# Six instead of eight heads of the recurrent layer computed ahead by Strassen's scheme, with reloads on GpSimd's queue and four gates in the recurrence's buffers

## The chip, the core and the metric

The kernel runs on one NeuronCore of a Trainium2 chip. TensorE (PE in the profile) multiplies matrices into PSUM, VectorE (DVE) and ScalarE (ACT) work element by element, GpSimd (POOL) and SyncE (SP) mostly issue DMAs. Each engine works through its own list of instructions strictly in order, and waits on semaphores for the others. The metric is the device time of one execution in microseconds (us).

## The reference, cut to what matters

A trunk of two residual layers runs over 528 positions (16 meta tokens and 512 inputs) of width 2048, in float32. Layer 0 is a convolution module beside a sparse attention; the change leaves its arithmetic alone. Layer 1 is a gated linear recurrence with 16 heads of width 128:

```python
def odd_mixer(hn, w_in, lb, norm_g, w_out):
    q, fz, i, g = split_last(hn @ w_in, (D_REC, D_REC, D_REC, D_REC))
    log_f = jnp.logaddexp(jnp.log(lb), jnp.log1p(-lb) + jax.nn.log_sigmoid(fz))
    k = (1.0 - lb) * jax.nn.sigmoid(-fz)
    o = hgrn2_chunkwise(heads(jax.nn.silu(q)), heads(log_f), heads(k), heads(i))
    o = o * lax.rsqrt(jnp.mean(jnp.square(o), -1, keepdims=True) + RMS_EPS)
    o = o * norm_g.reshape(H_C, DV_C).astype(jnp.float32)
    o = o.reshape(bsz, t_len, D_REC).astype(hn.dtype) * jax.nn.silu(g)
    return o @ w_out
```

So each head needs three projections of the normed input (its forget gate `fz`, its query `q`, its value `i`, called `v` in the kernel), then its recurrence; the output gate `g` is a fourth projection per head, and all heads go through one output projection.

## The kernel before, in words

**Products.** Every projection takes 128 output columns, a *stripe*, over 16 blocks of 128 inputs. A float32 operand is split into a high and a low part, and each block costs three matmuls: high by high (L177), weight high by input low (L178), weight low by input high (L179). The weights of half a stripe (8 blocks, 512 KB) come by one load: a DMA from SP into a staging tile `w32`, of which there are two (L144, `load_half`), then ScalarE rounds them to `wh` (L148) and VectorE takes the rest as `wl` (L149); there are three `wh` and three `wl`. A *wide* stripe covers all 528 positions in two parts of 264 columns: 2 halves x 2 parts x 8 blocks x 3 = 96 matmuls. A *narrow* stripe covers the 512 inputs with 48 matmuls of 512 columns.

**The stages of layer 1, in order of the program.**
1. The output projection of layer 0: 16 wide stripes. Behind each, VectorE adds the residual (L701), the sum goes to DRAM as `h1d` (L714), and the scaled sum `hg` becomes the input X1 of layer 1, split in two. For n >= 8, VectorE forms sums of two `hg` that Strassen's scheme needs, and two DMAs store them as `x1d` (L728, L729).
2. The Strassen stage. `fz` and `v` of the even heads are computed ahead for all positions: two stripes of the same head (a *pair*) times two halves of the positions form a 2x2 block product, done with 7 products of 24 matmuls (264 columns) instead of 8. Eight pairs give 56 products. Three sums of inputs, the forms N2, T3 and T4, come back from `x1d` through 24 reloads into three buffers `fr` (`reload`, L752), and are split by ScalarE (L189) and VectorE (L190); 8 more reloads restore X1 at the end. The products of pairs 0 to 2 run in the order (1, 5, 2, 3) for each pair, then all 6, 7 and 4, so N2 is first used by the 13th product, T3 by the 16th, T4 by the 19th. The sums of weights (four per pair) are made earlier, in DRAM, by copies and accumulating DMAs that are spread over layer 0 (`some_steps`, L241 and L243). The finished `fz` and `v` go to DRAM as `fvd` from GpSimd's queue (L803). Every third weight load of this stage, counted from its first, goes through a third staging tile `w33` (`strassen_weights`), which lies in the stage's own pool `fap`, in memory that other tiles held before.
3. The recurrence, head by head (`rec_head`). Even heads load `fz` and `v` back (L1011, L1012) and need only the narrow stripe of `q`; odd heads run three stripes. A head's own work on TensorE is many small matmuls (L859 to L861, L889, L893, L964 to L982, L993, L994) that wait for ScalarE and VectorE in a long chain; the stripes of later heads stand between them and fill the time. GpSimd clears a tile `vt` per head (L892), which waits until the head before the previous one has done its last L982, and then issues four DMAs of the sums for the output projection (L241, L243).
4. The 16 gates of layer 1, narrow stripes (`gate_on`): VectorE takes each from PSUM (L185), the result multiplies the head's output. Their tiles `gt2` lie in the pool `fp`, which opens when the recurrence's pool `hr` closes and takes its memory.
5. The output projection, 56 Strassen products of 256 columns, each load again through `strassen_weights`, with `w33` now in `fp`.

**What sets the order.** A scheduler builds each engine's list from priorities (`band`: weights before evacuations before the recurrence, stripes last) and its own estimate of when things are ready; a load that it expects to wait for memory can stand ahead of loads that are needed sooner.

Of the kernel before, what the change touches and what calls it, by code (L numbers as in the profile page):

```python
# [10 lines left out]
F32 = mybir.dt.float32  # L11
# [7 lines left out]
SEQ = 512  # L19
NM = 16  # L20
T = SEQ + NM
# [51 lines left out]
def trunk_kernel(ctx: ExitStack, tc: tile.TileContext, x: bass.AP, w: bass.AP, wukv: bass.AP,  # L73
# [171 lines left out]
    def product_weights(pair, m):  # L245
# [3 lines left out]

    PAIRS = [(S_FQV + 3 * h, S_FQV + 3 * h + 2) for h in range(0, 16, 2)]  # L250
    plain_steps = [("copy", m, pr) for pr in PAIRS for m in (7, 5)]
    steps = [(what, m, pr) for g in (0, 4)
             for what, m in (("add", 7), ("add", 5), ("copy", 6), ("add", 6), ("copy", 3), ("add", 3))
             for pr in PAIRS[g:g + 4]]

# [438 lines left out]
    for n in (8 * j + i for i in range(8) for j in range(2)):  # L694
# [26 lines left out]
        if n >= 8:  # L721
            with band(SIDE):

                a, b = first_hg, hg
                V.tensor_tensor(b[:, RT], b[:, RT], a[:, RT], op=OP.subtract)
                V.scalar_tensor_tensor(a[:, LT], b[:, RT], -1.0, a[:, LT], op0=OP.mult, op1=OP.subtract)
                V.scalar_tensor_tensor(b[:, LT], a[:, LT], -1.0, b[:, LT], op0=OP.mult, op1=OP.subtract)
                Q.dma_start(x1d[n - 8], a)  # L728
                Q.dma_start(x1d[n], b)  # L729
        if tap and n in (0, 15):  # L730
# [19 lines left out]
    def reload(i, sl):  # L750
        src = fap.tile([128, HT], F32, name="fr", bufs=3)
        Q.dma_start(src, x1d[i, :, sl])  # L752
        return src
# [9 lines left out]

    loads = [0]

    def strassen_weights(pair, m, pool):
        loads[0] += 1
        return load_half(product_weights(pair, m),
                         w32=pool.tile([128, 1024], F32, name="w33", bufs=1) if loads[0] % 3 == 0 else None)

    turns = [(p, m) for ms in ((1, 5, 2, 3), (6,), (7,), (4,)) for p in range(3) for m in ms]
    turns += [(p, m) for p in range(3, 8) for m in (1, 5, 2, 6, 7, 3, 4)]
    U, C = {}, {}
    for at, (pr, m) in enumerate(turns):
# [5 lines left out]
        with band(WGT):  # L780
            hi, lo = strassen_weights(PAIRS[pr], m, fap)
        products(o, hi, lo, forms1[FORM[m]], True, True)
# [247 lines left out]

    hr.__exit__(None, None, None)
    fp = ctx.enter_context(tc.tile_pool(name="fp", bufs=2, side="left", reuse_waits="tile"))
    HS = SEQ // 2
# [25 lines left out]

    def gate_on(h, ps):  # L1060
        t = gt2()
        g, th = t[:, :SEQ], t[:, SEQ:]
        with band(EVAC):
# [24 lines left out]

    for i in range(8):
        for h, forms_of in ((i, forms_of_first), (8 + i, forms_of_both)):  # L1090
            gate_on(h, stripe(S_G + h, X1, wide=False))
            with band(SIDE):
                forms_of(i)
    with band(SIDE):
# [69 lines left out]
    for at, (pr, m) in enumerate(turns):  # L1164
# [7 lines left out]
        with band(WGT):  # L1172
            hi, lo = strassen_weights(OPAIRS[pr], m, fp)
        issued = products(o, hi, lo, forms[FORM[m]], True, True)
# [123 lines left out]
```

## Time and profile before

| what | value |
|---|---|
| time, median of 3 runs (lowest, highest) | 1982.93 us (1981.18, 1988.01) |
| the profiled execution's own time | 1983.95 us |
| its span, first to last instruction | 1982.2 us |
| TensorE busy | 97% of the span |
| VectorE, ScalarE busy | 71%, 46% |
| mean granted TensorE clock | 0.988 |

The profile is of one execution. A row of a timeline has the start in us, the duration in us, the engine, the line, the operation, output<-inputs, shapes, the count, and in brackets the idle time before it and what ended that. A row of waits has engine and line, who released it, then us in total, times, and the longest. A row of a table of stretches has, for each engine, its busy us with the number of instructions in brackets, then the granted clock, the DMA share and GB/s; a few per cent of matmul records are missing from such counts.

### The profile page before, as it was taken

What the parts mean: (1) busy time and instruction counts of PE and PEld (TensorE: products, weight loads), DVE (VectorE), ACT (ScalarE), POOL (GpSimd) and SP (SyncE); (2) the same over time, 40 slices, a digit from 0 to 9 for tenths busy, and PEclk for the clock granted to TensorE, in tenths of its full rate; (3) what the DMA queues carried; (4) which work ended last, traced back from release to release, by engine and by line L of the source; (5) the groups of instructions that cost most, each with busy time, mean ns of one, the idle gap of its engine ahead of it and who ended that gap; (6) DMA issues with size and microseconds to landing.
All of it is one profiled execution on the core that took longest, in us unless ns stands there. A gap on an engine that the chain in (4) does not pass through costs nothing.

```text
span 1982.2 us, 36659 instructions
## 1 busy us (share of the span) xinstructions
PE 1921.8 (97%) x14806; PEld 1797.7 (91%) x14806; DVE 1409.3 (71%) x2685; ACT 903.2 (46%) x1603; POOL 163.5 (8%) x266
## 2 busy tenths in 40 slices
PE   9999999999999999998999999999999987999997
PEld 8999899999999999998999889988888866888997
DVE  6699989987375454444766877878878876558776
ACT  6332442234436433333534655556565653325554
POOL 1000001122230200000000200001000100000000
PEclk9999999999999999999999999999999997999999
DMA  6434335677774744444766745446454531326555
GB/s 229 149 120 141 123 105 130 163 175 184 180 190 129 186 135 162 157 166 143 255 224 205 213 137 160 129 123 165 118 160 108 161 101 54 96 90 203 186 189 172
DMA packets 96889, 308.05 MB, mean 155 GB/s; under 512 B 12432, under 2 KB 24248, under 8 KB 95696
## 3 DMA queue, kind: packets, MB, share of 16 engines
q1 hardware_dynamic: 75840, 228.16, 34.8%
q0 software_dynamic: 20592, 77.36, 17.4%
q8 instruction: 116, 1.90, 0.4%
q14 instruction: 53, 0.43, 0.1%
q10 hardware_dynamic: 288, 0.19, 0.0%
HBM read 277.91 MB, written 86.98 MB: 184 GB/s over the span
## 4 chain that ended last, share of the span: by engine, by line
PE 87%; issue 5%; DVE 3%; DMA 3%; ACT 1%; POOL 1%; SPq 0%; DVEq 0%; POOLq 0%; ACTq 0%
PE mps L177 22%; PE mps L178 22%; PE mps L179 22%; PE s L177 3%; PE s L179 3%; PE s L178 3%; DMA L<-bdram 2%; PE po L600 1%; PE s L860 1%; PE s L859 1%; PE s L861 1%; PE s L575 1%; DMA L<-mask 1%; PE po L981 1%; PE po L982 1%
## 5 line engine op out<-in xcount | busy, mean ns | idle before, releaser
L177 PE MATMUL mps<-xh,wh 128*128 128x264 f32 (+2 forms) x3160 | 980.3, 311 | 17.9 <-ACT wh L148 6.9
L179 PE MATMUL mps<-xh,wl 128*128 128x264 f32 (+2 forms) x3160 | 979.0, 310 | 0.0
L178 PE MATMUL mps<-xl,wh 128*128 128x264 f32 (+2 forms) x3160 | 978.2, 310 | 0.0
L177 PEld LDWEIGHTS mps<-xh,wh 128*128 128x128 f32 x3160 | 597.5, 189 | 48.8 <-ACT wh L148 7.3
L148 ACT ACTIVATE wh<-w 128x1024 fp32r<-128x1024 f32 x337 | 356.4, 1058 | 592.0 <-PE mps L178 484.5
L178 PEld LDWEIGHTS mps<-xl,wh 128*128 128x128 f32 x3160 | 597.1, 189 | 29.0 <-issue 0.6
L179 PEld LDWEIGHTS mps<-xh,wl 128*128 128x128 f32 x3160 | 597.2, 189 | 27.7
L149 DVE TENSOR_TENSOR wl<-w,wh 128x1024 fp32r<-128x1024 f32 x337 | 411.9, 1223 | 184.5 <-ACT wh L148 177.5
L544 DVE SCALAR_TENSOR_TENSOR z<-u,vec,z 128x528 f32<-128x528 f32 x240 | 180.5, 762 | 2.6
L177 PE MATMUL s<-xh,wh 128*128 128x256 f32 (+1 forms) x328 | 92.7, 283 | 0.1
L178 PE MATMUL s<-xl,wh 128*128 128x256 f32 (+1 forms) x328 | 92.7, 283 | 0.0
L179 PE MATMUL s<-xh,wl 128*128 128x256 f32 (+1 forms) x328 | 92.6, 282 | 0.0
L185 DVE TENSOR_TENSOR gt<-mps,rstd 128x264 f32<-128x264 f32 (+1 forms) x80 | 38.4, 481 | 74.9 <-PE mps L179 74.0
L243 POOL DMA_DIRECT2D ws<-in_w_dram x64 | 61.9, 1046 | 98.9 <-DMA ws<-ws 62.4
L855 ACT ACTIVATE qhm<-q 128x256 f16<-128x256 f32 x128 | 51.7, 414 | 38.0 <-DVE q L957 33.2
L177 PEld LDWEIGHTS s<-xh,wh 128*128 128x128 f32 x328 | 61.9, 189 | 0.5 <-ACT wh L148 0.4
L178 PEld LDWEIGHTS s<-xl,wh 128*128 128x128 f32 x328 | 61.7, 188 | 0.6 <-issue 0.6
L179 PEld LDWEIGHTS s<-xh,wl 128*128 128x128 f32 x328 | 61.7, 188 | 0.0
L856 DVE SCALAR_TENSOR_TENSOR qlm<-q,qhm 128x256 f16<-128x256 f32 x128 | 52.5, 419 | 11.9 <-ACT qhm L855 11.3
L942 DVE COPY_PREDICATED A<-msk,s 128x256 f32<-128x256 uint8 x96 | 46.7, 487 | 12.0 <-PE s L861 11.4
L855 ACT ACTIVATE kt0h<-k 128x512 f16<-128x512 f32 (+1 forms) x64 | 33.3, 520 | 41.4 <-PE s L861 21.4
L855 ACT ACTIVATE kt1h<-k 128x256 f16<-128x256 f32 x64 | 26.9, 420 | 54.3 <-DVE k L948 27.7
(401 smaller groups left out, 2905.6 us busy)
## 6 DMA issues: line engine op xcount, KB each, us to landing
w<-in_w_dram SPq DMA_DIRECT2D x275, 512.0 KB, 3.6
ws<-in_w_dram POOLq DMA_DIRECT2D x80, 512.0 KB, 6.8
w<-ws SPq DMA_DIRECT2D x64, 512.0 KB, 4.2
ws<-ws POOLq DMA_DIRECT2D x32, 512.0 KB, 4.7
ws<-in_w_dram SPq DMA_DIRECT2D x16, 512.0 KB, 5.0
hin<-in_x_dram SPq DMA_DIRECT2D x16, 264.0 KB, 3.9
h1d<-hin SPq DMA_DIRECT2D x16, 264.0 KB, 2.0
x1d<-hg SPq DMA_DIRECT2D x16, 264.0 KB, 3.3
```

Of the source, the lines that this page charges most:

```text
L148: S.activation(uh, used, AF.Copy)
L149: V.tensor_tensor(ul, used, uh.bitcast(F32), op=OP.subtract)
L177: P.matmul(o, hi[:, ws], xh, start=start and k == 0, stop=False)
L178: P.matmul(o, hi[:, ws], xl, start=False, stop=False)
L179: issued.append(P.matmul(o, lo[:, ws], xh, start=False, stop=stop and k == 7))
L185: V.tensor_tensor(dst[:, sl.start - o:sl.stop - o], p[:dst.shape[0]], rstd[:dst.shape[0], sl], op=OP.mult)
L243: return G.dma_start(wsum[pair, m], src, accum_op=OP.add, max_dma_last_dim=4096)
L544: eng.scalar_tensor_tensor(z, u[:, j:j + T], col(V_CW + i * CW + j), z, op0=OP.mult, op1=OP.add)
L575: P.matmul(p[:nq, :s1 - s0], qh[:, q0:q0 + nq], Kh[:, s0:s1], start=True, stop=True)
L855: S.activation(hi, src, AF.Copy, scale=scale)
L856: V.scalar_tensor_tensor(lo, src, scale, hi, op0=OP.mult, op1=OP.subtract)
L942: V.copy_predicated(A.rearrange("p b (n a m) -> p b n a m", a=2, m=mm)[:, :, :, 1, :], msk[:, li - 1 + i:li + i, :].rearrange("p b (n m) - ...
```

## The change

Four edits, all of layer 1.

1. `PAIRS` holds the heads 0, 2, ... 10 only: 42 Strassen products instead of 56. Heads 12 and 14 compute `fz` and `v` with plain wide stripes, as odd heads do. The sums of weights for the two pairs go away (4 copies on SP, and on GpSimd's queue 4 copies and 8 accumulating DMAs), and the rest is made in groups of 3 pairs instead of 4.
2. The stores of `x1d`, the 32 reloads `fr`, and the loads of `fz` and `v` of the ahead-computed heads move from SP's queue to GpSimd's.
3. `w33` takes every third load, but only from the 10th of each of the two Strassen stages on (product index over 6 and a multiple of 3); before, a counter ran through both stages, and `w33` took the 3rd, 6th, ... load of the first stage, and in the second the 1st, 4th, 7th and so on.
4. The first four gates (heads 0, 8, 1, 9) are written before the recurrence's pool closes, and put their result into its tiles `fz` and `v`. Their part in the forms for the output projection stays behind the closing, as for the other twelve.

```diff
+    AHEAD = range(0, 12, 2)
+    PAIRS = [(S_FQV + 3 * h, S_FQV + 3 * h + 2) for h in AHEAD]
...
-                Q.dma_start(x1d[n - 8], a)
-                Q.dma_start(x1d[n], b)
+                G.dma_start(x1d[n - 8], a)
+                G.dma_start(x1d[n], b)
...
     def reload(i, sl):
         src = fap.tile([128, HT], F32, name="fr", bufs=3)
-        Q.dma_start(src, x1d[i, :, sl])
+        G.dma_start(src, x1d[i, :, sl])
...
-    def strassen_weights(pair, m, pool):
-        loads[0] += 1
+    def strassen_weights(pair, m, pool, at):
+
+        own = at > 6 and at % 3 == 0
         return load_half(product_weights(pair, m),
-                         w32=pool.tile([128, 1024], F32, name="w33", bufs=1) if loads[0] % 3 == 0 else None)
+                         w32=pool.tile([128, 1024], F32, name="w33", bufs=1) if own else None)
...
-        if h % 2 == 0:
+        if h in AHEAD:
             with band(EVAC):
-                Q.dma_start(fz, fvd[h])
-                Q.dma_start(v, fvd[h + 1])
+                G.dma_start(fz, fvd[h])
+                G.dma_start(v, fvd[h + 1])
...
-        if h % 2:
+        if h not in AHEAD:
             ps = stripe(S_FQV + 3 * h + 2, X1)
...
+    gates = [h for i in range(8) for h in (i, 8 + i)]
+    for h in gates[:4]:
+        gate_on(h, stripe(S_G + h, X1, wide=False), ht([128, T], F32, "fz", 2)[:, :SEQ],
+                ht([128, T], F32, "v", 2)[:, :SEQ])
+    hr.__exit__(None, None, None)
+    fp = ctx.enter_context(tc.tile_pool(name="fp", bufs=2, side="left", reuse_waits="tile"))
```

The order of TensorE, VectorE and ScalarE is the same in both kernels up to the end of layer 0, and in the recurrence the same stripes stand between the same heads up to the end of head 8.

**SP's list where the Strassen stage begins**, before. `w33_10623` is the load of the third product, `w32_10655` and `w32_10690` are those of the fourth and fifth; `hg` are the tiles that the stores read; in brackets the semaphores that a DMA waits for.

```order
L714 DMA h1d_105<-hin1_10137 128x528 [waits DMAHW5_49,DVE_49]
L144 DMA w32_10655<-ws67_3_4202 128x1024 [waits DMAHW0_49,DMASW5_49,DVE_49]
L144 DMA w32_10690<-in_w_dram 128x1024 [waits DMAHW4_49,DVE_49]
L714 DMA h1d_105<-hin1_10265 128x528 [waits DMAHW1_49,DVE_49]
L728 DMA x1d_106<-hg_10251 128x528 [waits DVE_49]
L729 DMA x1d_106<-hg_10379 128x528 [waits DMAHW2_49,DVE_49,Activation_49]
L144 DMA w33_10623<-in_w_dram 128x1024 [waits DMAHW3_49,DMAHW2_49,DMAHW5_49,DMAHW0_49,Activation_49]
L752 DMA fr_10411<-x1d_106 128x264 [waits PE_49]
```

The same place after the change; `w32_10599` is the third product's load, `w33_10829` the tenth's, and the semaphores DMASW are those of DMAs from GpSimd's queue.

```order
L144 DMA w32_10599<-in_w_dram 128x1024 [waits DMAHW0_49,DVE_49]
L144 DMA w32_10631<-ws67_3_4126 128x1024 [waits DMAHW2_49,DMASW1_49,DVE_49]
L715 DMA h1d_105<-hin1_10241 128x528 [waits DMAHW1_49,DVE_49]
L144 DMA w32_10666<-in_w_dram 128x1024 [waits DMAHW4_49,DVE_49]
L144 DMA w32_10698<-ws73_5_1223 128x1024 [waits DMAHW5_49,DMASW2_49,DVE_49]
L144 DMA w32_10730<-in_w_dram 128x1024 [waits DMAHW7_49,DVE_49]
L144 DMA w33_10829<-ws79_5_1440 128x1024 [waits DMASW6_49,DMASW5_49,DMASW7_49,DMASW4_49,DMAHW3_49,DMASW3_49,DMAHW6_49,DMASW2_49,DMASW1_49]
L144 DMA w32_10762<-ws73_3_4147 128x1024 [waits DMAHW0_49,DVE_49]
L144 DMA w32_10797<-in_w_dram 128x1024 [waits DMAHW1_49,DVE_49]
```

The third load no longer waits for the stores of `x1d` and stands ahead of the fourth; the load that waits for them is now the tenth, and the eighth and ninth are queued behind it.

**TensorE's list in the last head's recurrence**, before: `po` is the head's output in PSUM, `st` its state, the L177 row the next gate stripe.

```order
L975 MATMUL s_19411<-vt,kk 128x128
L978 MATMUL s_19417<-vt,kk 128x128
L978 MATMUL s_19423<-vt,kk 128x128
L981 MATMUL po<-q,st 128x128
L978 MATMUL s_19429<-vt,kk 128x128
L982 MATMUL po<-A,vt 128x128
L981 MATMUL po<-q,st 128x128
L982 MATMUL po<-A,vt 128x128
L981 MATMUL po<-q,st 128x128
L982 MATMUL po<-A,vt 128x128
L993 MATMUL s_19443<-sh,ones_h 128x512
L994 MATMUL s_19443<-sl,ones_h 128x512
```

After the change, the same head, from its last but one state on.

```order
L981 MATMUL po<-q,st 128x128
L982 MATMUL po<-A,vt 128x128
L177 MATMUL mps<-xh,wh 128x512
L178 MATMUL mps<-xl,wh 128x512
L179 MATMUL mps<-xh,wl 128x512
L177 MATMUL mps<-xh,wh 128x512
L178 MATMUL mps<-xl,wh 128x512
L179 MATMUL mps<-xh,wl 128x512
```

Before, TensorE has no stripe left from the middle of head 14 to the end of head 15, with 13 gates still to come behind; after, gate matmuls stand between the pieces of both heads, and 9 gates are left behind the last head.

**GpSimd's list in the recurrence**, after the change, around the clearing of `vt` for head 9 (`vt_16109`): `ws` are sums of weights in DRAM, `v_16351` is the value of head 10.

```order
L243 DMA ws139_5_15798<-in_w_dram 128x1024 [waits DMASW6_49,DMASW0_49]
L892 MEMSET vt_16109 128x128 [waits PE_49,Activation_49]
L241 DMA ws139_6_16343<-ws139_5_15798 16x8192 [waits DMASW0_49]
L1012 DMA v_16351<-fvd_107 128x528 [waits DMASW2_49,PE_49]
L243 DMA ws139_6_16343<-in_w_dram 128x1024 [waits DMASW1_49]
L241 DMA ws139_3_16346<-ws139_6_16343 16x8192 [waits DMASW4_49,DMASW3_49]
L243 DMA ws139_3_16346<-in_w_dram 128x1024 [waits DMASW4_49]
L892 MEMSET vt_16434 128x128 [waits PE_49,Activation_49]
```

The load of head 10's value, which stood among the weight loads of SP, now stands behind a clearing that waits for head 7's end, and a copy that waits for an earlier sum.

More of the change, by code (lines that the diff above doesn't have):

```diff
@@ L247, in product_weights @@
         return {1: w[pair[0], 0], 2: w[pair[0], 1], 4: w[pair[1], 1]}[m] if m in (1, 2, 4) else wsum[pair, m]
-    PAIRS = [(S_FQV + 3 * h, S_FQV + 3 * h + 2) for h in range(0, 16, 2)]
+    AHEAD = range(0, 12, 2)
+    PAIRS = [(S_FQV + 3 * h, S_FQV + 3 * h + 2) for h in AHEAD]
     plain_steps = [("copy", m, pr) for pr in PAIRS for m in (7, 5)]
-    steps = [(what, m, pr) for g in (0, 4)
+    steps = [(what, m, pr) for g in (0, 3)
              for what, m in (("add", 7), ("add", 5), ("copy", 6), ("add", 6), ("copy", 3), ("add", 3))
-             for pr in PAIRS[g:g + 4]]
+             for pr in PAIRS[g:g + 3]]
     def some_steps(todo, n, behind):
@@ L762, in trunk_kernel @@
                 forms1[name].append((hi, lo))
-    loads = [0]
-    def strassen_weights(pair, m, pool):
-        loads[0] += 1
+    def strassen_weights(pair, m, pool, at):
+        own = at > 6 and at % 3 == 0
         return load_half(product_weights(pair, m),
-                         w32=pool.tile([128, 1024], F32, name="w33", bufs=1) if loads[0] % 3 == 0 else None)
+                         w32=pool.tile([128, 1024], F32, name="w33", bufs=1) if own else None)
     turns = [(p, m) for ms in ((1, 5, 2, 3), (6,), (7,), (4,)) for p in range(3) for m in ms]
-    turns += [(p, m) for p in range(3, 8) for m in (1, 5, 2, 6, 7, 3, 4)]
+    turns += [(p, m) for p in range(3, len(PAIRS)) for m in (1, 5, 2, 6, 7, 3, 4)]
     U, C = {}, {}
@@ L780, in trunk_kernel @@
         with band(WGT):
-            hi, lo = strassen_weights(PAIRS[pr], m, fap)
+            hi, lo = strassen_weights(PAIRS[pr], m, fap, at)
         products(o, hi, lo, forms1[FORM[m]], True, True)
@@ L1029, in trunk_kernel @@
             tap("on0", ON[0])
-    hr.__exit__(None, None, None)
-    fp = ctx.enter_context(tc.tile_pool(name="fp", bufs=2, side="left", reuse_waits="tile"))
     HS = SEQ // 2
@@ L1058, in gt2, with gate_on @@
         return fp.tile([128, 2 * SEQ], F32, name="gt2", bufs=2)
-    def gate_on(h, ps):
-        t = gt2()
-        g, th = t[:, :SEQ], t[:, SEQ:]
+    def gate_on(h, ps, g, th):
         with band(EVAC):
@@ L1087, in forms_of_both @@
         V.scalar_tensor_tensor(aj, a, -1.0, aj, op0=OP.mult, op1=OP.subtract)
[L1089 to L1093, printed above, removed]
+    for at, h in enumerate(gates):
+        if at >= 4:
+            t = gt2()
+            gate_on(h, stripe(S_G + h, X1, wide=False), t[:, :SEQ], t[:, SEQ:])
+        with band(SIDE):
+            (forms_of_first if h < 8 else forms_of_both)(h % 8)
     with band(SIDE):
@@ L1172, in trunk_kernel @@
         with band(WGT):
-            hi, lo = strassen_weights(OPAIRS[pr], m, fp)
+            hi, lo = strassen_weights(OPAIRS[pr], m, fp, at)
         issued = products(o, hi, lo, forms[FORM[m]], True, True)
```

## The prediction

> **What bounds the kernel now.** First the page's table of engines:
>
> ```profile
> PE 1921.8 (97%) x14806; PEld 1797.7 (91%) x14806; DVE 1409.3 (71%) x2685; ACT 903.2 (46%) x1603; POOL 163.5 (8%) x266
> ```
>
> TensorE is the bound. The span is 1982.2 us and the profiled execution took 1983.95, 1.0 over the median of 1982.93. So two things can move the time: the number of matmuls, and the places where TensorE stands or runs slowly. I asked for stretches around the edits:
>
> ```profile
> 930.00:940.00 10.00, 5.04 (x21) 4.73 (x22) 4.53 (x6) 3.89 (x6) 0.00 (x0) 0.68 0.56 181
> 1160.00:1280.00 120.00, 120.00 (x1044) 107.94 (x1043) 95.00 (x212) 70.14 (x128) 8.87 (x15) 1.00 0.49 139
> 1436.07:1603.18 167.11, 160.60 (x1375) 140.37 (x1375) 134.58 (x303) 95.31 (x180) 14.42 (x26) 1.00 0.49 135
> 1618.00:1660.00 42.00, 21.53 (x216) 19.04 (x212) 28.36 (x68) 18.63 (x40) 0.82 (x1) 0.68 0.15 37
> ```
>
> Each row has the stretch, its length, then the busy time of TensorE, its weight loads, VectorE, ScalarE and GpSimd, and the granted clock. Early in the recurrence (1160 to 1280) TensorE has no gap; late it has small ones, and in the 42 us after 1618 it is half idle at a granted clock of 0.68. The other hole is at 930, the start of the Strassen stage. What ends the waits, first for TensorE from 1436 to 1661, then for SP's queue from 1600 to 1680:
>
> ```profile
> PE s L859 <- ACT qhm L855: 13.7, 8, 3.8
> PE mps L177 <- DVE gt L185: 2.8, 1, 2.8
> ```
> ```profile
> SPq L144 <- PE s L994: 37.0, 1, 37.0
> ```
>
> The last two heads are a chain over ScalarE, VectorE and TensorE with nothing to fill it: three gates occupy the three PSUM buffers, their tiles `gt2` lie in the recurrence's memory, and SP holds a load for the output projection (it waits 37.0 us for the last head's L994) with gate weights queued behind it.
>
> **Prices.** Weight roundings pace TensorE, one per half stripe or product; output gates pace narrow stripes; clearings of `vt` mark the ends of heads.
>
> ```profile
> 757.30 1.06 ACT L148 ACTIVATE wh<-w 128x1024 fp32r<-128x1024 f32 x1 [1.86 <-PE mps L178]
> 915.70 1.06 ACT L148 ACTIVATE wh<-w 128x1024 fp32r<-128x1024 f32 x1 [2.74 <-PE mps L178]
> 1002.21 1.06 ACT L148 ACTIVATE wh<-w 128x1024 fp32r<-128x1024 f32 x1 [1.60 <-PE mps L178]
> 1078.06 1.06 ACT L148 ACTIVATE wh<-w 128x1024 fp32r<-128x1024 f32 x1 [1.84 <-PE mps L178]
> ```
> ```profile
> 1684.57 0.69 DVE L185 TENSOR_TENSOR gt<-mps,rstd 128x512 f32<-128x512 f32 x1 [3.51 <-PE mps L179]
> 1796.50 0.69 DVE L185 TENSOR_TENSOR gt<-mps,rstd 128x512 f32<-128x512 f32 x1 [3.46 <-PE mps L179]
> ```
> ```profile
> 1148.80 0.38 POOL L892 MEMSET vt<- 128x128 f32 x1 [13.62 <-PE po L982]
> 1259.29 0.20 POOL L892 MEMSET vt<- 128x128 f32 x1 [28.63 <-PE po L982]
> 1436.07 0.20 POOL L892 MEMSET vt<- 128x128 f32 x1 [11.34 <-PE po L982]
> ```
>
> From 757.30 to 915.70 are 27 half stripes: 5.867 us each, 0.1222 per matmul of 264. From 1002.21 to 1078.06 are 26 Strassen products: 2.917 each. From 1684.57 to 1796.50 are 10 gates: 11.19 each, 0.2331 per matmul of 512. Heads 0, 3 and 8 end at 1148.80, 1259.29 and 1436.07. Between the first two stand 352 matmuls of 264 and 192 of 512 in the list, 43.0 + 44.8 us, in 110.5 us without gaps: the rest, 22.7, is three heads' own work, 7.6 each when it is covered.
>
> **The change part by part.**
>
> *Products.* 14 fewer Strassen products: 14 x 2.917 = 40.8 us out. Four wide stripes in: 384 x 0.1222 = 46.9 in. Both are TensorE time on the path. Net +6.1: taken alone, this edit loses. The weight sums that go with it lay beside TensorE work; I count nothing for them, and no wait of layer 0 is known to hang on the eight missing accumulations.
>
> *Start of the Strassen stage.*
>
> ```profile
> 921.69 0.43 DVE L701 TENSOR_TENSOR hin<-mps,hin 128x264 f32<-128x264 f32 x1 [2.49 <-PE mps L179]
> 926.71 1.05 PE L208 MATMUL s<-acc,ones_d 128*128 128x264 f32 x4
> 934.82 0.59 PE L177 MATMUL mps<-xh,wh 128*128 128x264 f32 x1 [6.46 <-ACT wh L148]
> 941.03 0.43 DVE L789 TENSOR_TENSOR on<-u,mps 128x264 f32<-128x264 f32 x1 [1.70 <-PE mps L179]
> ```
>
> The last stripe ends at 921.7, the third product at 941.0. Three products and the row sums (L208) need 3 x 2.917 + 1.05 = 9.8 of these 19.3 us; 9.5 are lost: 6.46 waiting for the third weights, the rest at the low clock behind that. The cause is the load of `w33`, which waits until the last `x1d` store has left memory that it takes over. After the change the third load uses a free `w32`. The tenth now waits for those stores, but the loads ahead of it take turns in two tiles and are therefore spread over the products before it: by then the stores (the last issued at 927.60, 3.3 us to land, both rows below) are in DRAM since about 931. The loads behind it are due from about 933. I take the whole 9.5 off.
>
> *Reloads on GpSimd.*
>
> ```profile
> 927.60 0.32 SPq L729 DMA_DIRECT2D x1d<-hg  x1
> 930.35 1.37 SPq L752 DMA_DIRECT2D fr<-x1d  x3
> 938.75 1.54 SPq L752 DMA_DIRECT2D fr<-x1d  x3
> 980.05 0.32 SPq L752 DMA_DIRECT2D fr<-x1d  x1
> ```
> ```profile
> x1d<-hg SPq DMA_DIRECT2D x16, 264.0 KB, 3.3
> fr<-x1d SPq DMA_DIRECT2D x32, 132.0 KB, 3.7
> fvd<-on POOLq DMA_DIRECT2D x16, 264.0 KB, 3.1
> ```
>
> The 4th to the 24th reload took from 938.75 to 980.05, 2.07 each through three buffers. TensorE no longer stands, so the 19th product, the first with T4, starts at 921.7 + 1.05 + 18 x 2.917 = 975.3 and wants T4's last part some 2.5 later, 977.8. From 928.3 (behind the last store on GpSimd) and three at once, the 24th is issued at 928.3 + 21 x 2.07 = 971.8, lands at 975.5 and is split by 976.5. That is 1.3 us of slack; if a turn of three buffers takes 1 us longer from GpSimd, the 24th is 7 later and TensorE waits 5.7; nothing excludes a faster turn. I take +1.5 between 0 and 5.7, nearer to 0 because GpSimd's stores of twice the size land in 3.1.
>
> GpSimd writes its DMAs' descriptors itself, and the place for a doubt is whether VectorE holds it up:
>
> ```profile
> L803 POOL DMA_DIRECT2D fvd<-on x16: 539/539/606, 973.6 to 1100.5; - x16
> ```
>
> Sixteen stores issued from GpSimd in this very stage, with VectorE busy for most of it, took 539 ns at the median and 606 at most. The Trainium skill (SBUF — State Buffer, "SBUF: two separate sides", the "DVE blocks DMA" trap) says that VectorE's two-port modes lock GpSimd out of writing descriptors and advises the queues of SyncE or ScalarE. By its figures, some 0.62 us alone and 3.1 locked out, seven turns would be up to 17 longer, an estimate that would put the sum near 1965. By the row no lockout of more than 0.07 us is seen in 16 issues, 2.1 over 32 reloads and off the path.
>
> *The recurrence's end.*
>
> ```profile
> 1508.34 1.22 DVE L149 TENSOR_TENSOR wl<-w,wh 128x1024 fp32r<-128x1024 f32 x1
> 1633.49 0.60 PE L889 MATMUL s<-ident,v 128*128 128x128 f32 x4
> 1656.84 0.55 PE L994 MATMUL s<-sl,ones_h 128*128 128x512 f32 x1 [0.23 <-DVE sl L990]
> 1660.15 0.79 PE L177 MATMUL mps<-xh,wh 128*128 128x512 f32 x1 [2.76 <-DVE gt L185]
> 1807.49 0.28 PE L177 MATMUL mps<-eh,wh 128*128 128x256 f32 x1
> ```
>
> From head 8's end to the first product of the output projection are 1807.49 - 1436.07 = 371.4 us. What stands there is 432 matmuls of 264 (52.8), 960 of 512 (223.8) and seven heads (53.2): 329.8. So 41.6 are lost to gaps, low clock and uncovered chains. After the change 384 more matmuls of 264 and seven gates in all stand between the pieces of heads 9 to 15: in the last head alone 156 narrow matmuls, 36 us, around a chain that takes 24 alone (from L889 at 1633.5 to L994 at 1656.8). Kept are the end, where the eighth gate still waits for `gt2` (2.76, and 0.5 for L993 and L994), and small gaps: before 1603 they are 6.5 us in five heads, 1.3 each, where a head has one narrow stripe to cover it; the fuller list should halve that, 0.65 x 7 = 4.6. Kept 7.9, gained 33.7 (range 24 to 38).
>
> VectorE doesn't become the bound: from 1436 to 1603 it is busy 134.6 of 167 us; four more wide stripes add 8 weight rests of 1.22 and 8 evacuations of 0.43, 13 us, to heads that get 46.9 more of stripes on TensorE.
>
> *Entry of the output projection.* `w33` used to carry the 1st, 4th and 7th load; now the first nine share two tiles, with loads of the residual between them:
>
> ```profile
> 1802.62 2.70 SPq L1170 DMA_DIRECT2D on<-h1d  x6
> 1806.18 6.15 SPq L1170 DMA_DIRECT2D on<-h1d  x7
> 1825.59 0.39 PE L177 MATMUL mps<-xh,wh 128*128 128x256 f32 x1 [0.44 <-ACT wh L148]
> ```
>
> Before, only 0.44 us is lost here, so there is no cushion. One load more stands behind each block: I take +2.0, between 0 and a product's 2.9.
>
> *The sum.* 1983.95 - 40.8 + 46.9 - 9.5 + 1.5 - 33.7 + 2.0 = 1950.4; against the median, 1.0 less: **1949 us**, 1.7% faster.
>
> **The rivals.**
>
> *The chain stays the bound (0.13).* Gates stand between the pieces, but VectorE and ScalarE serve them too, so the chains of heads 12 to 15 stretch. For it: TensorE's longest wait is on ScalarE. Against it: VectorE is busy only 28.4 of the 42 us after 1618. If half of the 33.7 goes, 1966.
>
> *The start's hole moves (0.15).* The tenth load, or reloads from GpSimd, arrive late, and ScalarE, which has the splits among the roundings, holds the weights back. If the 9.5 stays, 1959. For it: 1.3 us of slack. The Trainium skill (DMA: Bandwidth & Descriptors, "Issuing engines are not separate DMA queues") says that spreading DMAs over engines saves only issue time: by that the move itself brings nothing. I agree as far as that goes: the gain comes from the load that no longer waits, not from the queue.
>
> *Slower: the sums starve the heads (0.04).* On GpSimd a head's value now stands behind a clearing that waits for an earlier head's end, and behind accumulations that wait for one another. If each of five reloads (heads 2 to 10) held its head by over 7 us, the gain of 33.6 would be gone, and at 10 each the time is 1949 + 50 = 1999. Against it:
>
> ```profile
> 1405.10 0.21 POOL L892 MEMSET vt<- 128x128 f32 x1 [27.08 <-PE po L982]
> 1409.82 0.80 POOL L243 DMA_DIRECT2D ws<-in_w_dram  x1 [3.77 <-DMA ws<-ws]
> 1469.55 0.20 POOL L892 MEMSET vt<- 128x128 f32 x1 [26.81 <-PE po L982]
> ```
>
> Head 9's clearing is at 1405.1; the load of head 10's value stands behind one copy, so at about 1406, and its transposes come when head 9 ends, 1469.5. The lead is some 60 us, and it decides only when that is used up.
>
> *Nothing to see (0.03).* The freed matmul time falls in the recurrence and the chains take it all: +6.1 - 9.5 and no gain at the end leaves 1980.
>
> **How the numbers follow.** A measurement here tells 0.3%, 6 us, from no change. The forecast's own case has 0.65: 1943 (end gains 38, no new stalls) to 1957. The rivals at 1959 and 1966 bring the range's upper end to 1963, which leaves out half of the chain's case, the slower one and the null. Faster 0.93, same 0.03, slower 0.04.
>
> **What would show it.** Right: no gap over 2 us between 921 and 945; 2.92 us per product and 42 of them; TensorE busy over 9 tenths through the last heads at clock 1.00, one wait of about 3 us for VectorE's `gt` behind the last head, then 9 gates of 11.2 us. SP's waits show no 37 us on L994. Wrong: waits of TensorE on `qhm` of over 10 us, ScalarE waiting on `fr` for over 3 us at a time, or L889 waiting on a DMA of `v`.

## The result and the profile after

The changed kernel takes **1952.21 us** (median of 4 runs, 1952.12 to 1956.98) against 1982.58 for the kernel before (median of 4): a ratio of 0.9848, interval 0.9824 to 0.9871, or 30.4 us less. The forecast was 1949. The profiled execution took 1952.31, its span is 1950.5, which is 31.7 shorter than before. TensorE is still the bound:

```profile
PE 1916.2 (98%) x14854; PEld 1794.6 (92%) x14854; DVE 1391.1 (71%) x2669; ACT 904.5 (46%) x1599; POOL 184.3 (9%) x310
```

A gain of 1.5% that comes from several places is read best from marks that both kernels have. From the timelines of the changed kernel: the last evacuation of layer 0, the first narrow stripe behind the Strassen stage, the clearings of `vt` at the ends of heads 0, 8 and 13, and the first product of the output projection.

```profile
918.54 0.43 DVE L702 TENSOR_TENSOR hin<-mps,hin 128x264 f32<-128x264 f32 x1 [2.49 <-PE mps L179]
1045.48 0.40 PE L177 MATMUL mps<-xh,wh 128*128 128x512 f32 x1
1099.83 0.38 POOL L892 MEMSET vt<- 128x128 f32 x1 [12.85 <-PE po L982]
1386.49 0.20 POOL L892 MEMSET vt<- 128x128 f32 x1 [9.72 <-PE po L982]
1569.49 0.21 POOL L892 MEMSET vt<- 128x128 f32 x1 [31.36 <-PE mps L178]
1772.76 0.28 PE L177 MATMUL mps<-eh,wh 128*128 128x256 f32 x1
```

The differences of such marks make the columns of this table (the fifth mark is not used there; `out` runs from the last mark to the end of the span, `rest` is everything behind layer 0). Every kernel of this study is in it; the experiments are described below.

| kernel | median us | ratio to before | layer 0 | Strassen | head 0 | heads 1-8 | head 8 to out | out | rest |
|---|---|---|---|---|---|---|---|---|---|
| before | 1982.58 | 1 | 921.7 | 173.8 | 53.3 | 287.3 | 371.4 | 174.7 | 1060.5 |
| **the change** | 1952.21 | 0.9848 | 918.5 | 126.9 | 54.4 | 286.7 | 386.3 | 177.7 | 1032.0 |
| change, all on SP's queue | 1954.25 | 0.9868 | 922.9 | 124.9 | 53.3 | 286.7 | 386.5 | 177.4 | 1028.7 |
| before + `w33` rule | 1978.01 | 0.9981 | 918.3 | 167.6 | 57.6 | 287.3 | 370.7 | 177.5 | 1060.6 |
| before + four gates | 1972.04 | 0.9950 | 919.9 | 173.3 | 53.3 | 287.3 | 360.5 | 174.7 | 1049.2 |
| before + six heads | 1973.04 | 0.9955 | 924.9 | 132.8 | 53.3 | 286.7 | 400.1 | 174.5 | 1047.4 |
| change, eight gates | 1948.18 | 0.9826 | 925.2 | 127.8 | 53.6 | 286.7 | 378.3 | 176.6 | 1022.9 |
| change, early `w33` in out | 1949.95 | 0.9848 | 920.0 | 125.9 | 54.1 | 286.7 | 385.8 | 175.2 | 1027.6 |
| change, five heads | 1959.30 | 0.9883 | 923.4 | 106.7 | 53.3 | 302.2 | 390.2 | 179.7 | 1032.1 |
| change, seven heads | 1955.85 | 0.9870 | 921.3 | 150.8 | 53.6 | 287.3 | 367.5 | 177.9 | 1037.0 |
| eight gates + early `w33` | 1948.26 | 0.9822 | 925.0 | 126.6 | 54.7 | 286.7 | 378.3 | 175.2 | 1021.4 |
| the same, all on SP | 1943.02 | 0.9796 | 922.9 | 125.4 | 53.3 | 286.7 | 378.3 | 174.5 | 1018.2 |
| change, four `fr` buffers | 1952.58 | 0.9846 | 918.6 | 125.1 | 54.7 | 286.7 | 386.9 | 178.5 | 1031.9 |
| the same on SP, `fz`, `v` on GpSimd | 1940.50 | 0.9788 | 925.8 | 125.0 | 53.7 | 286.7 | 378.3 | 174.8 | 1018.5 |

The columns come from one profiled execution each; each median and ratio comes from several, against the kernel before on the same chip, and their intervals reach 0.001 to 0.0025 to each side. One execution of eight gates with the early `w33` took 9497.56 us and is left out of that kernel's ratio; nothing here explains it. The columns scatter as well: the Strassen stage has the same code in the change, with eight gates, with the early `w33` and with both, and takes 125.9 to 127.8 us. Of the 31.7 us between the two spans, 46.9 are gained in the Strassen stage (40.8 of them are the products left out), 3.2 in layer 0 and 0.6 in heads 1 to 8; 14.9 are given back between head 8 and the output projection, where four wide stripes more have to be computed, 3.0 behind that and 1.0 in head 0.

The two holes of the prediction, in the changed kernel's tables of stretches. First the start of the Strassen stage:

```profile
930.00:940.00 10.00, 10.00 (x84) 10.00 (x84) 4.57 (x8) 3.61 (x7) 0.54 (x1) 1.00 0.72 245
940.00:950.00 10.00, 9.08 (x73) 8.66 (x72) 5.87 (x10) 4.87 (x8) 2.67 (x5) 1.00 0.71 232
980.00:990.00 10.00, 9.12 (x71) 8.64 (x70) 6.80 (x10) 4.41 (x5) 2.63 (x5) 1.00 0.73 240
```

Where TensorE was half idle at a clock of 0.68 it is now full at 1.00; two holes of 0.9 us have come up behind. Then the heads 9 to 13, the last two heads, and the 8 us behind the last head's L994:

```profile
1386.49:1569.49 183.00, 182.43 (x1664) 169.90 (x1665) 140.88 (x316) 102.51 (x187) 14.37 (x25) 1.00 0.47 130
1569.49:1663.85 94.36, 93.89 (x601) 75.69 (x600) 58.95 (x112) 46.69 (x76) 2.85 (x5) 1.00 0.34 101
1663.85:1671.85 8.00, 2.29 (x7) 1.50 (x6) 4.46 (x8) 6.89 (x11) 0.00 (x0) 0.72 0.37 127
```

Up to the end of the last head 1.0 us is idle in 277. Behind it stands one hole, larger than before. The waits of TensorE from 1386 on, and of SP's queue from 1560 to 1680:

```profile
PE mps L177 <- DVE gt L185: 5.7, 1, 5.7
...
PE s L859 <- ACT qhm L855: 0.5, 1, 0.5
```
```profile
SPq L144 <- DVE wl L149: 53.0, 8, 8.5
```

The 13.7 us on ScalarE's `qhm` are down to 0.5, and SP has no wait for L994 any more: its longest are the ordinary ones for a free staging tile.

### The profile page after: what moved, and what is told of

Same layout as the page of the kernel before. It is cut to its first block, busy times and chain, and to the rows that moved or that the text cites. A ratio compares the mean times of both kernels' runs of the same rounds, so it can differ in the third digit from the quotient of the medians.

```text
span 1950.5 us, 36684 instructions
## 1 busy us (share of the span) xinstructions
PE 1916.2 (98%) x14854; PEld 1794.6 (92%) x14854; DVE 1391.1 (71%) x2669; ACT 904.5 (46%) x1599; POOL 184.3 (9%) x310
## 4 chain that ended last, share of the span: by engine, by line
PE 81%; issue 7%; DMA 5%; DVE 3%; ACT 2%; POOL 1%; SPq 0%; POOLq 0%; DVEq 0%; ACTq 0%
PE mps L178 22%; PE mps L179 21%; PE mps L177 21%; PE s L179 2%; PE s L178 2%; PE s L177 2%; DMA fr<-x1d 1%; DMA ws<-in_w_dram 1%; PE po L601 1%; PE s L859 1%; PE s L860 1%; PE s L468 1%; PE s L861 1%; PE s L576 1%; PE po L981 1%
## 5 line engine op out<-in xcount | busy, mean ns | idle before, releaser
L177 PE MATMUL mps<-xh,wh 128*128 128x264 f32 (+2 forms) x3240 | 1002.3, 310 | 12.1 <-DVE gt L185 8.5
L179 PE MATMUL mps<-xh,wl 128*128 128x264 f32 (+2 forms) x3240 | 1001.0, 309 | 0.8 <-DVE wl L149 0.8
L178 PE MATMUL mps<-xl,wh 128*128 128x264 f32 (+2 forms) x3240 | 1001.0, 309 | 0.1
L177 PEld LDWEIGHTS mps<-xh,wh 128*128 128x128 f32 x3240 | 611.2, 189 | 42.5 <-DVE gt L185 9.1
L178 PEld LDWEIGHTS mps<-xl,wh 128*128 128x128 f32 x3240 | 610.8, 189 | 29.0 <-issue 1.2
L179 PEld LDWEIGHTS mps<-xh,wl 128*128 128x128 f32 x3240 | 610.5, 189 | 29.3 <-DVE wl L149 1.0
L148 ACT ACTIVATE wh<-w 128x1024 fp32r<-128x1024 f32 x331 | 350.1, 1059 | 578.3 <-PE mps L178 478.6
L149 DVE TENSOR_TENSOR wl<-w,wh 128x1024 fp32r<-128x1024 f32 x331 | 404.6, 1223 | 195.3 <-ACT wh L148 184.7
L178 PE MATMUL s<-xl,wh 128*128 128x256 f32 (+1 forms) x312 | 88.1, 282 | 0.0
L177 PE MATMUL s<-xh,wh 128*128 128x256 f32 (+1 forms) x312 | 87.9, 282 | 0.0
L243 POOL DMA_DIRECT2D ws<-in_w_dram x56 | 52.2, 1025 | 90.5 <-DMA ws<-ws 52.2
L178 PEld LDWEIGHTS s<-xl,wh 128*128 128x128 f32 x312 | 58.6, 188 | 0.6 <-issue 0.6
L177 PEld LDWEIGHTS s<-xh,wh 128*128 128x128 f32 x312 | 58.8, 188 | 0.0
L942 DVE COPY_PREDICATED A<-msk,s 128x256 f32<-128x256 uint8 x96 | 46.8, 487 | 10.9 <-PE s L861 10.7
L569 POOL DMA_DIRECT2D L<-mask x32 | 28.5, 891 | 211.7 <-DMA L<-bdram 127.6
```

The costliest lines, as they stand in the source:

```text
L148: S.activation(uh, used, AF.Copy)
L149: V.tensor_tensor(ul, used, uh.bitcast(F32), op=OP.subtract)
L177: P.matmul(o, hi[:, ws], xh, start=start and k == 0, stop=False)
L178: P.matmul(o, hi[:, ws], xl, start=False, stop=False)
L179: issued.append(P.matmul(o, lo[:, ws], xh, start=False, stop=stop and k == 7))
L243: return G.dma_start(wsum[pair, m], src, accum_op=OP.add, max_dma_last_dim=4096)
```

## The experiments

**The queue.** The five `G.dma_start` of the second edit went back to `Q.dma_start`:

```diff
-                G.dma_start(x1d[n - 8], a)
+                Q.dma_start(x1d[n - 8], a)
...
-        G.dma_start(src, x1d[i, :, sl])
+        Q.dma_start(src, x1d[i, :, sl])
...
-                G.dma_start(fz, fvd[h])
+                Q.dma_start(fz, fvd[h])
```

> The changed kernel with its first queue edit undone: the stores of x1d, the 32 reloads and the loads of fz and v are issued by SP again. The theory of the prediction: the move is worth next to nothing, since the 4th to the 24th reload took 1.95 us each from GpSimd (937.15 to 976.18 in the profile of the change) and 2.07 from SP (before): 1952.2, give or take 2, and the stage from the last stripe of layer 0 to its end stays at 126.9 us within 2. Rival A, the move pays: SP holds weight loads behind reloads that wait for a free buffer, the loads of the 8th and 9th product come late, and the hole of the stage's start is partly back: 1956 to 1961. Rival B, the move costs (GpSimd issues slower): 1949 or less, with the T4 stall of about 1 us gone.

1954.25 us, 2.0 over the change. But the marks say otherwise than the time:

```profile
922.87 0.43 DVE L702 TENSOR_TENSOR hin<-mps,hin 128x264 f32<-128x264 f32 x1 [2.49 <-PE mps L179]
1047.78 0.40 PE L177 MATMUL mps<-xh,wh 128*128 128x512 f32 x1
```

From the one to the other are 124.9 us, 2.0 less than in the change, and everything behind layer 0 is 3.2 shorter; layer 0, which has nothing of the move before its output projection, ended 4.3 later. So the move is no gain in the stage that it is for; what it does to the time was left to the last runs.

**The `w33` rule alone.** The kernel before, with the product's index instead of the running counter:

```diff
-         w32=pool.tile([128, 1024], F32, name="w33", bufs=1) if loads[0] % 3 == 0 else None)
+         w32=pool.tile([128, 1024], F32, name="w33", bufs=1) if own else None)
```

> The kernel before with the renumbering of w33 alone (from the 10th product of each stage, every third). The theory: the hole of 9.4 us at the stage's start is the third load's wait for the stores; without it about 6 are gained there net (late reloads of T4 take 1 to 3 of it back), and the entry of the output projection, with no third tile for its first nine loads, costs 2 to 3: 1976 to 1980, TensorE's wait of 6.5 us for the third weights gone from the trace. Rival: the hole moves to the 10th load, which now stands in SP's list ahead of loads needed sooner and waits for the same stores and reloads: no gain at the start, 1983 to 1986, with one wait of over 4 us for weights between 930 and 960.

1978.01 us (ratio 0.9981, interval 0.9971 to 0.9990): 4.3 less. The wait of 6.5 us is gone and the stage is 6.2 shorter, as the theory has it, and the output projection 2.8 longer. What the expectation lacks is head 0, which takes 57.6 instead of 53.3 and has a wait that the kernel before lacks there (its lines are two lower than those of before):

```profile
PE s L857 <- ACT qhm L853: 2.1, 1, 2.1
```

So behind layer 0 nothing is left of this edit in this profile (1060.6 against 1060.5); its layer 0 is 3.4 shorter. But the profiled execution took 1980.66, 2.7 over its median, so the late head 0 may be of this execution alone, and the 4.3 in the medians may in part be the edit's. Why head 0 is late here and not in the change wasn't settled.

**Four gates alone, six heads alone.** Each on the kernel before, with the lines of the diff that belong to it:

```diff
+    for h in gates[:4]:
+        gate_on(h, stripe(S_G + h, X1, wide=False), ht([128, T], F32, "fz", 2)[:, :SEQ],
+                ht([128, T], F32, "v", 2)[:, :SEQ])
```
```diff
+    AHEAD = range(0, 12, 2)
...
-        if h % 2 == 0:
+        if h in AHEAD:
```

> The kernel before with four gates in the recurrence's tiles alone. The theory: the hole at the recurrence's end (21.5 us of idle TensorE between 1603 and 1661, and the low clock with it) is for lack of matmuls that may run, and four gates of 11.2 us fill most of it: 16 to 20 us gained, 1963 to 1967; small gaps before 1603 stay. Rival A: the hole is filled by the two heads that go back to plain stripes, not by gates; then this edit alone gains under 8: over 1975. Rival B: SP holds the gates' weights behind the load that waits for the last head (37.0 us on L994), so the gates can't start although their tiles are free: 1980 to 1983, with the same 37 us in SP's waits and TensorE waiting for gate weights.

> The kernel before with six heads ahead instead of eight alone (SP's queue, the old w33, all gates after the recurrence). The theory: 14 products out and 4 wide stripes in cost 6.1, the hole at the end stays, since nothing new may run beside the last head, the small gaps of heads 9 to 14 (some 6.5 us) mostly go, and layer 0 gains about 3 as it did in the change: 1978 to 1982, a change within noise, and 9 products' worth of gates behind the last head as before. Rival: the stripes of heads 12 and 14 push later work towards the end and fill the last hole too: 1960 to 1968. Second rival, on layer 0: its 3 us (921.7 to 918.5 at its end) have nothing to do with the weight sums; then layer 0 ends at 921 to 922 here.

1972.04 and 1973.04 us: 10.3 and 9.3 less than before. Both expectations missed, in opposite directions: the gates fill 10.9 us between head 8 and the output projection (371.4 to 360.5) where 16 to 20 were expected; the two heads bring 46.9 us of wide stripes and the stretch grows by 28.7 only, so they fill 18.2 where some 6 were expected. That is the rival of the second expectation in kind, though not in size. The tables of stretches show where, from head 8's end to head 13's and from there to the last L994; of the kernel before the second stretch (the first stands in the prediction), then both with gates alone and with six heads alone:

```profile
1603.18:1656.84 53.66, 34.94 (x312) 29.85 (x312) 37.66 (x88) 25.24 (x54) 2.87 (x5) 0.78 0.27 69
```
```profile
1433.79:1606.46 172.67, 166.29 (x1401) 145.13 (x1402) 135.94 (x306) 95.95 (x180) 14.40 (x26) 1.00 0.49 134
1606.46:1686.99 80.53, 69.14 (x479) 56.17 (x477) 52.87 (x105) 44.53 (x74) 2.87 (x5) 0.94 0.33 92
```
```profile
1397.70:1580.69 182.99, 182.42 (x1664) 169.90 (x1665) 140.81 (x316) 102.52 (x187) 14.41 (x25) 1.00 0.48 130
1580.69:1647.35 66.66, 54.37 (x410) 44.74 (x408) 43.83 (x93) 30.43 (x59) 2.87 (x5) 0.87 0.32 87
```

In the last two heads TensorE idled 18.7 us before (53.66 less 34.94), at a clock of 0.78. With gates it idles 11.4 at 0.94; with the heads' stripes 12.3 at 0.87, and the 6.5 us of gaps in heads 9 to 13 go as well (0.6 is left). A list that is fuller earlier pushes stripes back: with six heads alone 116 narrow matmuls stand between the ends of heads 13 and 14 in TensorE's list, before 29, and none beside the last head in either. With gates alone only 13 stand beside the last head, where the change has 156, and SP still holds a load for L994, as rival B of the first expectation has it, though TensorE waits for no weights there:

```profile
SPq L144 <- PE s L994: 15.8, 1, 15.8
```

Together they give 32.1 (46.9 less the 14.9 of the result), 3.0 more than the sum of the two.

**Eight gates.** `gates[:4]` became `gates[:8]`, and `at >= 4` became `at >= 8`:

> The changed kernel with eight gates instead of four in the recurrence's tiles fz and v. In its list TensorE has 163 narrow matmuls in the last head instead of 156, so nothing more is filled there. The theory: what is left behind the last head is the wait of 5.7 us for VectorE's gt, whose tile gt2 lies in memory that the recurrence frees at its end, and a clock of 0.81 around it; with tiles that are free earlier this wait goes: 1945 to 1949. Rival A: the wait is only renamed, since the eighth gate needs a tile that an earlier gate still holds, or is held by the chain on VectorE: 1951 to 1953. Rival B: the pool that takes the recurrence's memory opens later, its first forms come late and the output projection starts late: 1954 or more.

1948.18 us. The 8 us behind L994, and the stretch from head 8 is 8.0 shorter (378.3):

```profile
1672.20:1680.20 8.00, 8.00 (x36) 6.47 (x35) 3.70 (x5) 4.67 (x5) 0.00 (x0) 1.00 0.27 76
```

The wait is gone, not renamed. Behind layer 0 the profile is 9.1 shorter than the change's; the median shows 4.0. Layer 0 ended 6.6 later in this profile, at 925.2, with the very same list of instructions up to there as the change.

**The third tile in the output projection.** The rule became `at % 3 == 0 and (at > 6 or pool is not fap)`:

> The changed kernel with the third staging tile used in the output projection from its first product on (the 1st, 4th, 7th load, as before), and unchanged in the first Strassen stage. The theory: the output projection lost 3.0 us by the change (174.7 to 177.7 from its first product to the end) because its first nine loads share two tiles; here it is 174.7 again and the time 1949 to 1950. Rival: the load in w33 is queued on SP ahead of the last gates' weights and waits for the last head, as for 37.0 us before, and the gates behind it start late: the wait at the recurrence's end grows by 3 or more and the time is 1952 or more.

1949.95 us, and the output projection takes 175.2 instead of 177.7. The tables of stretches from its first product on, of the change and of this run:

```profile
1772.76:1950.00 177.24, 163.93 (x1353) 162.76 (x1351) 127.63 (x217) 92.24 (x140) 0.00 (x0) 0.96 0.58 193
```
```profile
1772.36:1947.00 174.64, 162.09 (x1353) 161.13 (x1351) 127.52 (x217) 91.80 (x140) 0.00 (x0) 0.98 0.60 196
```

The same 1353 matmuls take 1.8 us less, at a clock of 0.98 and not 0.96. No wait on SP for the last head came back.

**Five and seven heads.** `range(0, 10, 2)` and `range(0, 14, 2)`; with seven, the sums of weights are made in groups of four pairs again, as before:

> The changed kernel with five heads computed ahead instead of six (7 products less, 2 wide stripes more). The theory: the holes of the recurrence's end are nearly used up (9.6 us are left, 5.7 of them a wait that no stripe can fill), so the trade of 3.0 us a head that the plain stripes cost is paid in full: 1954 to 1957. Rival: more stripes go on filling: a head brought 9 us when two were taken back in the kernel before (end 18.2 us shorter than the stripes added), and one more would bring at least 4: 1951 or less.

> The changed kernel with seven heads computed ahead (7 products more, 2 wide stripes less). Its list has 85 narrow matmuls in the last head where the change has 156. The theory: the trade of products and stripes gives 3.0, and the holes at the end come back in part, 71 narrow matmuls or 16.5 us less beside a chain of about 24 us: 4 to 10 us lost: 1953 to 1959. Rival: 85 narrow matmuls (20 us) cover the last head's chain well enough, and the gates alone do the work: 1948 to 1950.

1959.30 and 1955.85 us. With five, the stage is 20.2 shorter and the stretches from head 0's end to the output projection together 19.4 longer: two more wide stripes (23.5) fill another 4.0, but the rest comes out even (1032.1), and no expectation holds in full: in the profiles the whole difference is layer 0 (923.4 against 918.5). With seven, `rest` is 5.0 longer; 4.7 of it are holes come back between head 8 and the output projection (18.8 shorter for 23.5 less of stripes), in the range expected; that its stage grew by 23.8 and not by 20.4 was not expected. TensorE waits there for the splits of the reloads, which it doesn't in the change, and the clock between 980 and 1000 is 0.91 where the change has 1.00:

```profile
PE s L177 <- ACT fh L189: 2.4, 2, 1.8
```

Why the splits come later here is open, and this profile is of its longest run, 4.3 over the median. Six is the least of the three by the time; behind layer 0, five and six can't be told apart.

**Both improvements, and the queue again.** First eight gates with the early `w33`, then the same with all DMAs of the second edit on SP, and four buffers for the change:

```diff
-        src = fap.tile([128, HT], F32, name="fr", bufs=3)
+        src = fap.tile([128, HT], F32, name="fr", bufs=4)
```

> The changed kernel with eight gates in the recurrence's tiles and the third staging tile from the first product of the output projection on, both together. The theory: the two act at different places, the wait behind the last head (8.0 us from head 8's end to the output projection in the profile with eight gates) and the output projection's entry (2.5): together 10.5 from the change's stages, so a time of 1952.2 less 8 to 10: 1942 to 1946. Rival: with the gates' weights sooner in SP's list, the w33 load ahead of them waits for memory of the recurrence, and the two together give no more than eight gates alone: 1947 to 1949.

> As the run before, with the stores of x1d, the reloads and the loads of fz and v on SP's queue again. The theory: on SP the Strassen stage and head 0 were 3.1 us shorter in the profile (124.9 + 53.3 against 126.9 + 54.4), and the 2 us by which the time was longer came from the output projection of layer 0 and the scatter of layer 0 (its end at 922.9 against 918.5): the same time as with GpSimd's queue within 1.5 us, with a stage of 124 to 126 us. Rival A: the queue move is a real gain of 2: this is 2 slower. Rival B: the move is a loss of 3: this is 3 faster.

> The changed kernel with four buffers fr for the reloads instead of three. The theory: of the 3.4 us that the Strassen stage loses now, about 1 is the late T4 (the 24th reload issued at 976.2, TensorE's waits at 983.5 and 984.5) and 1 the late weights at 942.9 to 944.2, which ScalarE rounds behind splits; a fourth buffer brings the reloads forward by one turn of some 2 us and takes the first away: a stage of 125.5 to 126.5 us and a time within 1.5 us of the change. Rival: the reloads compete with weight loads for ScalarE's turn, and bringing them forward makes the weights later: a stage of 127 to 130 us.

1948.26, 1943.02 and 1952.58 us. The first missed by the time, which lies where the rival put it, but not by the rival's cause: both savings are in the marks (378.3 and 175.2), and behind layer 0 it is 10.6 shorter than the change, as the theory has it. Layer 0 was late again (925.0), and eight gates alone had already 1.2 of the output projection's 2.5 in their profile. The second stands with rival B: behind layer 0 it is 3.1 shorter than the first, as the first pair of this kind was by 3.2; the other 2 of the 5.2 us between their medians are layer 0. The medians alone would not say so, since those of the first pair differ by 2.0 the other way. The third bears out the theory of the late reloads: the stage takes 125.1 us from GpSimd with a fourth buffer, 1.8 less than in the change and 0.7 less than the shortest with three, yet neither the time nor all that stands behind layer 0 moves (1031.9 against 1032.0), since head 0 and the stretches behind head 8 are longer by as much; why wasn't settled.

```profile
918.63 0.43 DVE L702 TENSOR_TENSOR hin<-mps,hin 128x264 f32<-128x264 f32 x1 [2.49 <-PE mps L179]
1043.76 0.40 PE L177 MATMUL mps<-xh,wh 128*128 128x512 f32 x1
```

**Only `fz` and `v` on GpSimd.**

> As the run with eight gates, the third tile from the output projection's first product on and everything on SP's queue (1943.0), but with the loads of fz and v on GpSimd, as the change has them. It parts the 5.2 us between that run and the same with the whole queue move (1948.3). Theory: the parts seen in the traces are small and add up: the stage (reloads, 1.2 us) and head 0 (fz and v, 1.4 us); with fz and v alone on GpSimd, head 0 takes 54.3 to 54.7 and the time is 1944 to 1945. Rival A: most of the 5.2 is not the move but layer 0, which ended at 925.0 and 922.9 there and at 918.5 to 925.2 in other executions with the same list of instructions: 1943 give or take 1 if layer 0 ends near 923, and up to 4 more where it ends later. Rival B: later heads too are held by loads that GpSimd issues behind other work: head 0's end to head 8's is then over 287.5 us, where all runs but one (whose stripes are placed otherwise) had 286.7 to 287.3.

1940.50 us (1938.14 to 1946.11), ratio 0.9788, interval 0.9774 to 0.9801: 0.6% below the change. It is the lowest median here, but its interval overlaps that of the same with everything on SP (0.9784 to 0.9809), and behind layer 0 the two are equal (1018.5 and 1018.2). So `fz` and `v` cost nothing that the marks show on either queue, and the 2.9 us by which the whole move is longer than this run behind layer 0 go with the stores and reloads. Its profile is of its longest run, with layer 0's end at 925.8:

```profile
925.82 0.43 DVE L702 TENSOR_TENSOR hin<-mps,hin 128x264 f32<-128x264 f32 x1 [2.49 <-PE mps L179]
```

## Why the prediction was right, and where its steps were off

*Products and wide stripes (+6.1).* They hold: behind the holes, products still come every 2.92 us (15 of them between the weight roundings at 995.96 and 1039.74).

*Start of the Strassen stage (-9.5, and +1.5 for the reloads).* The stage lost 9.4 before (173.8 less 56 x 2.917 and 1.05) and loses 3.4 now; 6.0 were gained, 8.0 forecast (5.2 to 7.1 by the scatter of that stage). The mechanism was right: with six heads, SP's queue and the old rule the stage takes 132.8 us, with the new rule (and the gates, which come later) 124.9, which is 7.9 of the 9.5. Mis-sized was the reloads' term, "1.3 us of slack":

```profile
926.88 1.60 POOL L753 DMA_DIRECT2D fr<-x1d  x3
934.19 1.06 ACT L148 ACTIVATE wh<-w 128x1024 fp32r<-128x1024 f32 x1 [4.63 <-DMA w<-in_w_dram]
937.15 0.54 POOL L753 DMA_DIRECT2D fr<-x1d  x1 [8.67 <-DVE fl L190]
941.80 1.06 ACT L148 ACTIVATE wh<-w 128x1024 fp32r<-128x1024 f32 x1 [2.62 <-DMA w<-in_w_dram]
976.18 0.54 POOL L753 DMA_DIRECT2D fr<-x1d  x1 [0.47 <-DVE fl L190]
981.48 2.95 ACT L148 ACTIVATE wh<-w 128x1024 fp32r<-128x1024 f32 x3 [1.97 <-PE s L178]
983.54 0.39 PE L177 MATMUL mps<-xh,wh 128*128 128x264 f32 x1 [0.44 <-ACT wh L148]
```

I had the reloads turn at 2.07 us from the first one on. The first turn took 10.3: the split that frees a buffer stands in ScalarE's list behind a rounding that waited 4.63 us for its weights to land. My own rows could have told me, since the first turn took 8.4 before the change too (930.35 to 938.75). After it they turned at 1.95 (20 reloads from 937.15 to 976.18). The 24th left at 976.2, where the forecast, moved to this layer 0's end, has 968.7: 7.5 late, the slack used up. TensorE waits at 983.5 for weights whose rounding had itself stood until the matmuls with T4 (`s L178`) were done with theirs. With a fourth buffer the 24th leaves at 967.5 and that wait isn't there; the other hole, 942.9 to 944.2, stays, since its rounding at 941.80 waits for weights to land. SP's queue takes 1.2 to 2.0 of what is left away, a fourth buffer 1.8.

On GpSimd's descriptors the trace agrees with the row that the prediction went by:

```profile
L753 POOL DMA_DIRECT2D fr<-x1d x32: 536/536/543, 926.9 to 1037.4; - x32
```

The Trainium skill (SBUF — State Buffer, "SBUF: two separate sides") tells of GpSimd locked out while VectorE runs in its two-port modes. Here 32 issues took 536 to 543 ns with VectorE busy in 55 of the 80 us from 920 to 1000: no lockout is seen. Nothing here shows which of VectorE's instructions, if any, ran in such a mode, so the rule itself wasn't tested. Its advice, SyncE's or ScalarE's queue, was right all the same, by some 3 us behind layer 0; why is open, beyond that an issue takes 0.54 us from GpSimd and 0.32 at the least from SP.

*The recurrence's end (-33.7).* Measured 32.1. The sum was right. The split that I put on it for the experiments was wrong: I gave the gates the last hole and the two heads the small gaps; alone they are worth 10.9 and 18.2, and the last hole was filled in part by either. What was kept is 9.5 instead of 7.9. The prediction kept the wait for `gt2` at 2.76; it measured 5.7, and the rows of ScalarE between L994 and the gate, with TensorE's that follows, say why:

```profile
1663.59 1.06 ACT L148 ACTIVATE wh<-w 128x1024 fp32r<-128x1024 f32 x1 [3.85 <-PE mps L178]
1664.66 1.28 ACT L215 ACT_TABLE_LOAD   x1
1665.96 0.69 ACT L215 ACTIVATE rs<-s,eps_r 128x512 f32<-128x512 f32 x1
1666.66 1.28 ACT L216 ACT_TABLE_LOAD   x1
1667.96 0.63 ACT L216 ACTIVATE rs<-rs 128x512 f32<-128x512 f32 x1
1669.96 0.79 PE L177 MATMUL mps<-xh,wh 128*128 128x512 f32 x1 [5.71 <-DVE gt L185]
```

Gates between the heads put tanh (L1061) between the functions of the heads' norm, so ScalarE loads its tables twice in the very chain that TensorE waits for. From L994 to L996 it took 4.77 us (1663.85 to 1668.62), before 1.97 (1656.84 to 1658.81). The Trainium skill (ScalarE: Activation LUTs, "What ACT_TABLE_LOAD costs") gives 1.28 us for the load and 1.38 for a drain; the 1.28 agrees, but two loads made the chain 2.8 longer, and no drain shows: each load begins within 0.02 us of the end of what stands before it, and the next activation within 0.02 us of the load's end. I hadn't looked which functions an engine switches between when work is interleaved. Eight gates keep the loads and hide them under a gate.

*Entry of the output projection (+2.0).* Measured 3.0, of which 2.5 go with the early tile.

*Head 0 (no term).* 1.0 longer; with `fz` and `v` on GpSimd and the reloads on SP it is 0.4 longer than before.

*Layer 0 (0).* Measured -3.2, and nothing shows that it is the change's: six heads alone, with the same sums of weights as the change, ended it at 924.9, later than before. With the same instructions up to there, layer 0 ended at 921.7, 918.3 and 919.9 in the profiles of before, of the `w33` rule and of the gates alone, and at 918.5, 920.0, 925.2 and 925.0 in those of the change, of the early `w33`, of eight gates and of both. The waits of TensorE in layer 0's attention differ with it (480 to 600; the change, then eight gates):

```profile
PE s L594 <- ACT L L585: 0.3, 1, 0.3
```
```profile
PE s L594 <- ACT L L585: 3.1, 1, 3.1
```

So luck in layer 0 covered part of what the other steps missed: behind layer 0 the change is worth 28.5 us, where my sum has 33.6. What sets layer 0's length stays open, and so does whether it goes with the execution or with the program: the last run's times spread over 8.0 us, but eight gates with the early `w33`, late in its profile, took 1946.18 or more in every run, while the change was at 1952.1 to 1952.3 in three of four. That it goes with the bias loads of the attention, for which ScalarE's `L` waits, was only argued.

*The rivals.* None came. The chains don't stretch (0.5 us on `qhm`), GpSimd's sums don't starve a head (heads 1 to 8 take 286.7 against 287.3), and the start's hole moved only in part.

## What to carry to other kernels

A hole at the end of a chain is filled by whatever makes the list before it fuller, so price the fillers together and test them apart. Read a change of 1% from marks that both kernels have, and from several executions, since an untouched stage differed here by up to 7 us between profiles, as much as most of the parts. When work of another kind is put between the steps of a chain, look at what state the engine has to switch.

## What the hardware showed unexpectedly

The same list of instructions gave a layer 0 of 918.5 to 925.2 us in the profiles of four kernels. ScalarE loads function tables 13 times in the change and 7 times before, 1.28 us each, because gates stand between the heads. Reloads of 132 KB cost GpSimd 0.54 us each to issue and SP 0.32 at the least; with three buffers in turn, the Strassen stage of six heads took 125.9 to 127.8 us from GpSimd in four kernels and 124.9 to 125.4 from SP in three.
